# Second model of a fused two-model kernel: the last rows of w_out and of the down projection, two residual norms, the outputs and the first two feed-forward blocks go token tile by token tile

## The chip, the cores and the metric

The kernel runs on one core of one Trainium2 chip. What counts is the time of one execution on the device in microseconds (us), median of the runs shown. The profile is one execution more, taken by the hardware profiler. Engines are named as in the profile: PE (TensorE), DVE (VectorE), ACT (ScalarE), POOL (GpSimd), SP (the queue that issues the loads of weights).

## The reference, cut to what matters

256 tokens of width 1024 go through two models of two layers each. The first model (adaptive modulation, three attention mixers, a convolutional feed-forward part) is not edited. A layer of the second model, cut to the parts that are:

```python
for l in range(DEPTH):
    h = rms_norm_2(x, norm_mix_pre[l])
    proj = h @ w_in[l]                      # latents, rope key, branches, gates
    ...
    merged = ...                            # gated sum of four branches
    x = x + rms_norm_2(merged @ w_out[l], norm_mix_post[l])
    h = rms_norm_2(x, norm_ffn_pre[l])
    u, g = jnp.split(h @ w_ffn_in[l], 2, axis=-1)      # 2 x 2816 columns
    x = x + rms_norm_2((silu(u) * g) @ w_ffn_out[l], norm_ffn_post[l])
```

## The kernel before

The 256 tokens are two tiles of 128. x lies token-major in SBUF, the normed x feature-major. Every matrix product is done on exact float32r parts: a = ah + al, and `mm3` (L178, L179, L180) adds ah·bh, ah·bl and al·bh. "Product" below is one such pass, one PE instruction. Weights come by SP's DMA into `wraw` tiles of 128x1024 (5 buffers); ACT casts the high part into `wh` (L259) and DVE subtracts to get the low part `wl` (L260), 5 buffers each. With a gain, a split is L262 on ACT and L263 on DVE.

No order of work is written out by hand. A scheduler takes the program as it is written, with its dependencies and buffers, and gives every engine one fixed list; an engine waits at the head of its list. `HOLD` names norms whose splits are to stand ahead of splits of weights: of the pieces that come behind the first `free`, `held` are issued only after the norm's split numbered `at`.

The places that the change and the prediction touch:

- Handover from w_out to the feed-forward part ("out to ffn", once a layer) and from the down projection to the next layer ("gpre", once). Both run the norm `add_normed` of the projection's output: sums of squares on ACT (L216), gain times accumulator on DVE (L1370), `rsqrt` on DVE (L189 to L202, 128x1 steps), addition to x (L1375), sums of squares of the new x, a second `rsqrt`, x times r (L232 on DVE, L233 on ACT), 8 transposes a tile on PE (L236), splits L262 and L263. The accumulators are four banks: two named acc for tile 0, ada and o for tile 1.
- The feed-forward part: 22 blocks of 128 hidden columns, weights stationary and 256 tokens moving, 48 products for the gate half and the value half each; silu L1348, product with the value half L1349.
- The end: the last norm, then two output DMAs (L1408) of 512 KB.
- Latents (behind gpre): 48 products into two acc banks, sums of squares L1030, the rope key's 48 products and its DVE steps L1023 and L1024, an `rsqrt` of 128x4 steps (L189, L207 to L211), L1036 times r, transposes L1043. None of these lines is edited.

Of the kernel before, what the change touches and what calls it, by code (L numbers as in the profile page):

```python
# [15 lines left out]
AF = mybir.ActivationFunctionType  # L16
# [29 lines left out]
# norms whose splits go ahead of the weight splits emitted before: of the pieces behind the first `free`, `held` are issued  # L46
# only after the split numbered `at`
HOLD = dict(n11=(4, 6, 7), n20=(2, 6, 7), n21=(4, 6, 7), gpre=(2, 6, 7), gffn=(4, 6, 7))


class Core:
# [16 lines left out]
    # tag: (columns, slots) of the small and the short-lived tiles, which lie side by side in one; those of a block share their place  # L68
# [20 lines left out]
    def tile(self, shape, dtype, tag):  # L89
        """a tile of a ring"""  # L90
# [13 lines left out]
    BUFS = dict(T=20, xo=5, wraw=5, wh=5, wl=5, v4=3)  # L104

    def wide(self, tag, dtype=F32):
        """a [P, 1024] tile"""
        self.n += 1
        return self.pool.tile([P, 1024], dtype, tag=tag, name=f"{tag}_{self.n}", bufs=self.BUFS[tag])

    def pair(self):
        """two [P, 512] tiles side by side"""
        t = self.wide("T", F32R)
        return t[:, :512], t[:, 512:]
# [33 lines left out]
    def queue(self, ins, before):  # L148
        """ins is issued after before, on the same engine"""
# [3 lines left out]
    def weights(self, flat, key, layer, k0, nk, starts, width, piece=1024):  # L153
        """columns (start, k, col) of a weight block as exact (high, low) float32r parts"""
# [27 lines left out]
    def rsqrt(self, parts, n, inv_n):  # L182
        """(sum(parts) * inv_n + EPS) ** -0.5, n columns"""
# [12 lines left out]
        # a cubic step and Newton's, each short of a factor: s goes from -1 to -8/3 to 1024/27, which cancels big ** -0.5  # L196
# [22 lines left out]
    def norm_to(self, x, dst, col, gain, shift=None, sums=None, site=None, tiles=((0, 1),)):  # L219
        """x: two token-major [P, D] tiles -> dst[k] = (h, l) feature-major at columns col..col+256, rms-normed, *gain (+shift).  # L220
        sums: per tile, sums of squares of x's parts where these are already there."""
        self.norm_split(self.normed(x, sums), dst, col, gain, shift, site, tiles)

    def normed(self, x, sums=None):
        """rms-normed x, feature-major, in banks of two blocks"""
# [29 lines left out]
    def split(self, src, h, l, gain=None, shift=None):  # L255
        """src (PSUM or SBUF, fp32) * gain + shift -> h + l."""
# [15 lines left out]
    def transpose_split(self, blocks, dsts):  # L272
        """blocks: SBUF [P, P] pieces -> dsts (h, l) [P, P * len(blocks)]"""
# [8 lines left out]
class Block1:  # L282
# [22 lines left out]
    def ada(self, l):  # L305
        """modulation rows of a layer, a bank of four 512-column chunks at a time: [sh1|sc1], [gt1|sh2], [sc2|gt2];
        a chunk's rows lie at partitions 32g (x, 16 copies) and 32g + 16 (ctx). Yields after each step."""
# [38 lines left out]
    def mod_col(self, v, gain=None):  # L346
        """[P, 2, 4, 32] view (PSUM) -> per stream [P, 8]: the values, or (1 + values) * gain"""
# [11 lines left out]
    def gate_rows(self, l, n, s):  # L359
        """a stream's gate 1 or 2 on every partition, [P, 1024]"""  # L360
# [7 lines left out]
    def tables(self, l):  # L368
        """rope tables with the gains: t = q * TA + swap(q) * TB on (first half, second half) dims."""
# [49 lines left out]
    def in_chunk(self, l, name, XT, full):  # L419
        """256 columns of x @ w_in: per stream a psum view [P, 2 token tiles, 256]"""  # L420
# [14 lines left out]
    def qk(self, kind, ps, nh, hd, s):  # L435
        """One stream's q or k heads, psum view [P, 2, nh*hd]: rms norm, rope and gain, then exact (high, low) parts, feature-major
        and stacked on the partitions so that few passes hold all terms of (qh + ql)(kh + kl) but ql kl:
          q 64: [qh; ql] (or [ql; qh] where the head's kl lies in the upper half), k 64: [kh; kh] and pairs of kl,
          q 32: [qh; ql; qh], k 32: [kh; kh; kl].
        Tiles hold two heads of 256 tokens each."""  # L440
# [81 lines left out]
    def scores(self, q, k, unit):  # L522
        """psum [P queries, 512]: one x token tile against all 512 keys, or two ctx tiles against the 256 ctx keys each.
# [373 lines left out]
class Block2:  # L897
# [94 lines left out]
    def layer(self, l):  # L992
# [331 lines left out]
        for u in range(0, KD, 2):  # L1324
            out_proj(u)
# [218 lines left out]
```

## Time and profile before

| | |
|---|---|
| three runs | 2209.02, 2211.74, 2217.74 us; median 2211.74 |
| the profiled execution, first to last instruction | 2206.8 us: 4.9 below the median, 2.2 below the fastest run |
| PE busy | 2121.0 us (96%) |
| DVE busy | 1491.9 us (68%) |
| ACT busy | 1073.9 us (49%) |
| mean granted TensorE clock | 0.976 of full speed |

The profiled execution's own time is its span. A clock of 1.00 is the level of 2.4 GHz and 0.50 that of 1.2 GHz; a mean in between is the share of a stretch at either.

### The profile page before, as it was taken

Reading aid. Unit: us, or ns where it says so; the run is one execution under the profiler, and the core shown is the slowest. Engines: PE = TensorE matmul, PEld = TensorE weight load, DVE = VectorE, ACT = ScalarE, POOL = GpSimd, SP = SyncE. Lnnn points to the kernel's source line nnn. Section 1 sums busy time; section 2 is a strip of 40 time slices with the busy share of each in tenths; the row PEclk is TensorE's granted clock in tenths of the full one; section 3 lists DMA queues with packets and bytes.
Section 4 is the critical chain, followed back from the end, with each engine's and each line's share of the span. In section 5 each row is a group of like instructions: output and inputs, shape, how many; then the busy total and the mean of one; then the engine's idle time right before and its main releaser. Section 6 shows DMA issues by size and latency. Waiting matters only on the chain.

```text
span 2206.8 us, 35818 instructions
## 1 busy us (share of the span) xinstructions
PE 2121.0 (96%) x14204; PEld 1859.2 (84%) x14204; DVE 1491.9 (68%) x3008; ACT 1073.9 (49%) x1841; POOL 0.8 (0%) x7
## 2 busy tenths in 40 slices
PE   6999999899999999998999999998998999998998
PEld 3785667788888898788998899998997999997997
DVE  5663556855556686678777889866555879976454
ACT  4443453532333364566556644455444654454443
POOL 0000000000000000000000000000000000000000
PEclk9998999899999998999999999999999999999999
DMA  9344555322323331034554445554553545554662
GB/s 342 110 163 138 187 189 177 136 76 97 108 77 124 104 99 53 25 123 164 176 200 160 153 163 192 191 182 145 190 184 127 172 153 163 184 190 145 189 183 76
DMA packets 94839, 331.63 MB, mean 150 GB/s; under 512 B 10928, under 2 KB 11312, under 8 KB 94544
## 3 DMA queue, kind: packets, MB, share of 16 engines
q1 hardware_dynamic: 94672, 329.35, 45.5%
q8 instruction: 111, 1.82, 0.3%
q14 instruction: 56, 0.46, 0.1%
HBM read 328.20 MB, written 1.11 MB: 149 GB/s over the span
## 4 chain that ended last, share of the span: by engine, by line
PE 91%; DVE 6%; ACT 2%; DMA 1%; issue 1%; DVEq 0%; ACTq 0%
PE ps L178 17%; PE ps L179 17%; PE ps L180 16%; PE acc L178 6%; PE acc L179 6%; PE acc L180 6%; PE ps L533 4%; PE ada L318 3%; PE o L574 2%; PE ps L558 2%; PE ada L179 1%; PE ada L178 1%; PE ada L180 1%; PE o L179 1%; PE o L178 1%; PE o L180 1%
## 5 line engine op out<-in xcount | busy, mean ns | idle before, releaser
L178 PE MATMUL ps<-T,wh 128*128 128x256 f32 (+1 forms) x2640 | 787.4, 299 | 1.1 <-ACT T L262 1.1
L179 PE MATMUL ps<-T,wh 128*128 128x256 f32 (+1 forms) x2640 | 785.8, 298 | 0.4 <-DVE T L263 0.4
L180 PE MATMUL ps<-T,wl 128*128 128x256 f32 (+1 forms) x2640 | 784.5, 298 | 0.0
L260 DVE TENSOR_TENSOR wl<-wraw,wh 128x1024 fp32r<-128x1024 f32 (+1 forms) x514 | 608.8, 1201 | 157.6 <-ACT wh L259 90.8
L259 ACT CAST wh<-wraw 128x1024 fp32r<-128x1024 f32 (+1 forms) x514 | 515.8, 1031 | 234.6 <-PE ps L179 77.4
L178 PEld LDWEIGHTS ps<-T,wh 128*128 128x128 f32 x2640 | 506.1, 192 | 18.5 <-ACT T L262 2.1
L179 PEld LDWEIGHTS ps<-T,wh 128*128 128x128 f32 x2640 | 506.4, 192 | 17.3 <-DVE T L263 1.3
L180 PEld LDWEIGHTS ps<-T,wl 128*128 128x128 f32 x2640 | 506.2, 192 | 13.8
L178 PE MATMUL acc<-wh,T 128*128 128x256 f32 (+1 forms) x988 | 314.2, 319 | 3.5 <-ACT T L265 3.1
L179 PE MATMUL acc<-wl,T 128*128 128x256 f32 (+1 forms) x988 | 313.1, 318 | 2.3 <-DVE wl L260 2.3
L180 PE MATMUL acc<-wh,T 128*128 128x256 f32 (+1 forms) x988 | 311.5, 316 | 0.3 <-DVE T L269 0.3
L178 PEld LDWEIGHTS acc<-wh,T 128*128 128x128 f32 x988 | 190.3, 193 | 19.4 <-ACT T L265 3.5
L180 PEld LDWEIGHTS acc<-wh,T 128*128 128x128 f32 x988 | 189.9, 192 | 14.7 <-DVE arena L189 1.3
L179 PEld LDWEIGHTS acc<-wl,T 128*128 128x128 f32 x988 | 190.6, 193 | 13.9 <-DVE wl L260 3.0
L542 DVE TENSOR_REDUCE arena<-ps 128x1 f32<-128x512 f32 (+1 forms) x100 | 67.5, 686 | 78.9 <-PE ps L533 78.5
L1141 DVE SCALAR_TENSOR_TENSOR arena<-arena 128x241 f32<-128x241 f32 (+14 forms) x240 | 113.2, 474 | 3.7
L259 ACT CAST T<-arena 128x256 fp32r<-128x256 f32 (+2 forms) x128 | 58.8, 468 | 96.3 <-PE ps L179 26.7
L533 PEld LDWEIGHTS ps<-T,T 128*128 128x128 f32 (+2 forms) x320 | 59.3, 200 | 54.1 <-issue 29.2
L533 PE MATMUL ps<-T,T 128*128 128x256 f32 (+2 forms) x320 | 100.9, 386 | 2.1 <-ACT T L517 2.1
L318 PE MATMUL ada<-wraw,arena 128*32 128x512 f32 x384 | 86.9, 636 | 11.6 <-DVE arena L293 8.3
L546 ACT ACTIVATE arena<-ps,arena 128x512 f32<-128x512 f32 (+1 forms) x120 | 73.6, 620 | 48.1 <-DVE arena L542 37.5
L260 DVE TENSOR_TENSOR T<-arena,T 128x256 fp32r<-128x256 f32 (+2 forms) x128 | 63.2, 501 | 48.8 <-ACT T L259 48.4
(226 smaller groups left out, 2219.1 us busy)
## 6 DMA issues: line engine op xcount, KB each, us to landing
wraw<-w SPq DMA_DIRECT2D x586, 512.0 KB, 4.0
wraw<-w SPq DMA_DIRECT2D x22, 256.0 KB, 2.9
xo<-row SPq DMA_DIRECT2D x12, 256.0 KB, 6.2
v<-xin SPq DMA_DIRECT2D x4, 512.0 KB, 8.5
arena<-rpb SPq DMA_DIRECT2D x8, 256.0 KB, 2.7
v<-post SPq DMA_DIRECT2D x4, 512.0 KB, 4.4
arena<-bada SPq DMA_DIRECT2D x6, 256.0 KB, 5.4
arena<-bc SPq DMA_DIRECT2D x2, 768.0 KB, 4.0
```

The costliest lines, as they stand in the source:

```text
L178: mm(out, ah, bh, start=start, stop=False)
L179: mm(out, ah, bl, start=False, stop=False)
L180: mm(out, al, bh, start=False, stop=stop)
L259: a = nc.scalar.copy(h, src)
L260: b = nc.vector.tensor_tensor(l, src, h.bitcast(F32), op=ALU.subtract)
L318: nc.tensor.matmul(ps[32 * g : 32 * g + 32, :], self.cT[:, k].rearrange("p s r -> p (s r)"), raw[g // 2][0][:, g % 2 * 512 : g % 2 * 512 + ...
L533: self.nc.tensor.matmul(ps[:, col : col + 256], a[:, c], b, start=(n == 0), stop=(n == len(q[s]) - 1))
L542: nc.vector.tensor_reduce(m, ps.rearrange("p (t k) -> p t k", t=nt), axis=AX, op=ALU.max, negate=True)
L546: nc.scalar.activation(p[:, c], ps[:, c], AF.Exp, bias=m[:, i : i + 1], accum_out=tot[:, i : i + 1])
L558: nc.tensor.transpose(ps[:, b * P : b * P + P], p[:, b * P : b * P + P], K.ident)
L574: self.nc.tensor.matmul(out[64 * i : 64 * i + 64, t * P : t * P + P], v[:, k, cols[i] : cols[i] + 64], pts[i][:, b * P : b * P + P], start ...
L1141: yield v.scalar_tensor_tensor(y[:, lo:hi], zs[j][:, lo + t - 15 : hi + t - 15], self.cfw[:, j, t : t + 1], y[:, lo:hi], op0=ALU.mult, op1 ...
```

## The change

- `rows`, a new method, does the last four row blocks of w_out and of the down projection together: 24 products for token tile 0, then 24 for tile 1, and of the last two row blocks those of the first column half before those of the second. Before, two row blocks went at a time, tile 0 and tile 1 by turns.
- `add_normed` takes the sums of squares of a tile directly ahead of that tile's norm, and in the last layer sends each half of a tile out by a DMA of its own (four of 256 KB).
- The feed-forward norm's splits go tile by tile (16 of 128 columns where 8 of 256 were), and its `HOLD` entry follows.
- The first two feed-forward blocks are done together and token-major: normed tokens stationary, 256 weight columns moving, 48 products for tile 0, then 48 for tile 1; silu and product per tile, two transposes a tile (L1345) bring the result back.
- `wh` and `wl` have 7 buffers where 5 were, in both models.

The lines of the diff that do something (the rest removes comments):

```diff
-HOLD = dict(n11=(4, 6, 7), n20=(2, 6, 7), n21=(4, 6, 7), gpre=(2, 6, 7), gffn=(4, 6, 7))
+HOLD = dict(n11=(4, 6, 7), n20=(2, 6, 7), n21=(4, 6, 7), gpre=(2, 6, 7), gffn=(4, 4, 15))
-    BUFS = dict(T=20, xo=5, wraw=5, wh=5, wl=5, v4=3)
+    BUFS = dict(T=20, xo=5, wraw=5, wh=7, wl=7, v4=3)
...
-        for u in range(0, KD, 2):
+        for u in range(0, KD - 4, 2):
             out_proj(u)
+        out_proj(KD - 4, 4)
         sums = self.add_normed(acc, 0)
-        K.norm_to(x, H, 0, sm["gffn"], sums=sums, site="gffn")
+        K.norm_to(x, H, 0, sm["gffn"], sums=sums, site="gffn", tiles=((0,), (1,)))
...
+        get = [K.weights(wname, "w_ffn_in_2", l, 0, KD, [c], 256) for c in (0, FT * P)]
+        ft = K.bank()
+        for t in range(2):
+            ps = K.bank()
+            for i in range(2):
+                for k in range(KD):
+                    h, lo = H[k]
+                    K.mm3(ps[:, i * 256 : i * 256 + 256], (h[:, t * P : t * P + P], lo[:, t * P : t * P + P]), get[i](k * 256, 256), k == 0, k == KD - 1)
+            s = K.tmp()
+            act(s[:, :256], ps[:, :256], AF.Silu)
+            v.tensor_tensor(s[:, 256:], s[:, :256], ps[:, 256:], op=ALU.mult)
+            for j in range(2):
+                nc.tensor.transpose(ft[:, j * 256 + t * P : j * 256 + t * P + P], s[:, 256 + j * P : 256 + j * P + P], K.ident)
...
-            if j % 2 == 1 and j >= 3:
+            if j % 2 == 1 and j < FT - 1:
                 down(j - 3)
-        down(FT - 2)
+        down(FT - 4, 4)
+    def rows(self, acc, wname, key, X, a, n, last):
+        K = self.K
+        get = [K.weights(wname, key, self.l, a + i, 2, [0], 1024) for i in range(0, n, 2)]
+        order = [(f, cc) for f in range(n - 2) for cc in range(2)] + [(f, cc) for cc in range(2) for f in (n - 2, n - 1)]
+        for t in range(2):
+            c = slice(t * P, t * P + P)
+            for f, cc in order:
+                h, lo = X[a + f]
+                K.mm3(acc[t, cc], (h[:, c], lo[:, c]), get[f // 2](f % 2 * 1024 + cc * 512, 512), a + f == 0, a + f == last - 1)
...
-        parts = [[K.sumsq(acc[t, cc]) for cc in range(2)] for t in range(2)]
         for t in range(2):
-            tm = []
+            parts, tm = [], []
             for cc in range(2):
+                parts.append(K.sumsq(acc[t, cc]))
...
+                else:
+                    nc.sync.dma_start(self.ap["out"][t * P : t * P + P, c], xc)
```

What the change does to the engines' lists is seen at three places. The first is DVE's list at out to ffn of the second layer; the names are those above, ada and o being tile 1's accumulators. Before:

```order
L1370 TENSOR_TENSOR arena<-ada_19427,v_2316_19573 128x512
L1375 SCALAR_TENSOR_TENSOR arena<-arena 128x512 x2
L1370 TENSOR_TENSOR arena<-o_19428,v_2316_19573 128x512
L189 TENSOR_SCALAR arena<-arena 128x1 x2
L191 SCALAR_TENSOR_TENSOR arena<-arena 128x1 x2
```

After the change (L1390 and L1396 are the former L1370 and L1375):

```order
L1390 TENSOR_TENSOR arena<-ada_19448,v_2317_19594 128x512
L189 TENSOR_SCALAR arena<-arena 128x1
L1390 TENSOR_TENSOR arena<-o_19449,v_2317_19594 128x512
L191 SCALAR_TENSOR_TENSOR arena<-arena 128x1
L200 SCALAR_TENSOR_TENSOR arena<-arena 128x1
L197 TENSOR_SCALAR arena<-arena 128x1
L201 SCALAR_TENSOR_TENSOR arena<-arena 128x1
L198 SCALAR_TENSOR_TENSOR arena<-arena 128x1
L202 SCALAR_TENSOR_TENSOR arena<-arena 128x1
L199 SCALAR_TENSOR_TENSOR arena<-arena 128x1
L232 TENSOR_SCALAR xo_19632<-arena 128x512
```

Tile 0's second `rsqrt` (of its new x) has moved forward among tile 1's first steps: here L200, L201, L202 and L232 are tile 0's, and its L189 to L199 stand directly ahead of the first row. Before, the two tiles' `rsqrt` went in pairs.

The second place is PE's list of the second layer after the change, at the end of tile 0's 48 products of the first two feed-forward blocks (ps_19735 is tile 0's bank, ps_19788 tile 1's, ps_19734 the transposes'):

```order
L178 MATMUL ps_19735<-wh_19730,T_19631 128x256
L179 MATMUL ps_19735<-wl_19731,T_19631 128x256
L180 MATMUL ps_19735<-wh_19730,T_19631 128x256
L1345 MATMUL ps_19734<-arena 128x128 x2
L178 MATMUL ps_19788<-wh_19714,T_19628 128x256
```

Tile 0's two new transposes stand directly behind its products and ahead of tile 1's. All 16 transposes L236 of the norm stand ahead of the first product, as before.

The third place is DVE's list behind gpre of the second layer, at the latents' `rsqrt`, which no edited line touches. Before:

```order
L260 TENSOR_TENSOR wl_16496<-wraw_16489,wh_16495 128x1024
L189 TENSOR_SCALAR arena<-arena 128x4
L207 TENSOR_SCALAR arena<-arena 128x4
L209 TENSOR_TENSOR arena<-arena 128x4
L210 SCALAR_TENSOR_TENSOR arena<-arena 128x4
L211 SCALAR_TENSOR_TENSOR arena<-arena 128x4
L209 TENSOR_TENSOR arena<-arena 128x4
L260 TENSOR_TENSOR wl_16504<-wraw_16499,wh_16503 128x1024
L210 SCALAR_TENSOR_TENSOR arena<-arena 128x4
L211 SCALAR_TENSOR_TENSOR arena<-arena 128x4
```

After the change:

```order
L260 TENSOR_TENSOR wl_16529<-wraw_16522,wh_16528 128x1024
L207 TENSOR_SCALAR arena<-arena 128x4
L260 TENSOR_TENSOR wl_16694<-wraw_16689,wh_16693 128x1024
L209 TENSOR_TENSOR arena<-arena 128x4
L210 SCALAR_TENSOR_TENSOR arena<-arena 128x4
L260 TENSOR_TENSOR wl_16698<-wraw_16691,wh_16697 128x1024
L211 SCALAR_TENSOR_TENSOR arena<-arena 128x4
L209 TENSOR_TENSOR arena<-arena 128x4
L1023 TENSOR_TENSOR arena<-ps_16410,arena 128x512
L210 SCALAR_TENSOR_TENSOR arena<-arena 128x4
L1024 TENSOR_TENSOR arena<-arena 128x256
L211 SCALAR_TENSOR_TENSOR arena<-arena 128x4
```

In the shown part three subtractions stand where one stood, with the rope key's two steps among them; a fourth (wl_16706) follows the last row, ahead of the last three steps of the `rsqrt` and of L1036. Before, L1023, L1024 and the next subtraction stood behind L1036. The first layer's list has changed in the same way.

## Rows read from the trace of the kernel before

**Rows 1.** The page: engines' busy time, and the chain that ended last, by engine.

```profile
PE 2121.0 (96%) x14204; PEld 1859.2 (84%) x14204; DVE 1491.9 (68%) x3008; ACT 1073.9 (49%) x1841; POOL 0.8 (0%) x7
...
PE 91%; DVE 6%; ACT 2%; DMA 1%; issue 1%; DVEq 0%; ACTq 0%
```

**Rows 2.** Waits of PE: waiting line, releaser, us in total, times, longest.

```profile
PE ps L236 <- DVE arena L189: 20.9, 3, 7.4
```

**Rows 3.** Windows: stretch, length, busy time of each engine, granted clock, DMA.

```profile
851.00:864.40 13.40, 12.23 (x35) 7.20 (x34) 3.40 (x7) 3.14 (x7) 0.00 (x0) 0.65 0.07 20
905.70:915.40 9.70, 9.70 (x66) 6.71 (x65) 5.79 (x16) 4.71 (x11) 0.00 (x0) 1.00 0.06 20
1191.90:1200.00 8.10, 4.16 (x19) 3.58 (x20) 6.52 (x28) 4.96 (x15) 0.00 (x0) 0.79 0.37 115
1692.50:1705.00 12.50, 5.71 (x22) 4.92 (x22) 10.24 (x41) 8.03 (x24) 0.00 (x0) 0.59 0.18 54
1997.40:2012.20 14.80, 6.86 (x31) 6.46 (x32) 11.87 (x41) 8.31 (x22) 0.00 (x0) 0.65 0.33 107
```

**Rows 4.** Timeline at out to ffn, second layer: start, us, engine, line, [idle before].

```profile
1997.51 0.60 ACT L216 ACTIVATE arena<-o 128x512 f32<-128x512 f32 x1
...
2000.36 0.68 DVE L1370 TENSOR_TENSOR arena<-o,v 128x512 f32<-128x512 f32 x1
...
2002.87 1.41 DVE L1375 SCALAR_TENSOR_TENSOR arena<-arena 128x512 f32<-128x512 f32 x2
```

**Rows 5.** Timeline of PE at the same place.

```profile
2004.73 1.97 PE L236 MATMUL ps<-arena,xo 128*128 128x128 f32 x8 [7.36 <-DVE arena L189]
2007.31 1.97 PE L236 MATMUL ps<-arena,xo 128*128 128x128 f32 x8 [0.61 <-DVE xo L232]
2008.93 0.56 PE L178 MATMUL ps<-T,wh 128*128 128x256 f32 x1
```

**Rows 6.** Groups of the tile ps, 1505 to 1520 us: duration ns min/median/max.

```profile
L1348 ACT ACTIVATE arena<-ps x2: 384/384/384, 1512.3 to 1517.3; 128x256 f32<-128x256 f32 x2
L1349 DVE TENSOR_TENSOR arena<-arena,ps x2: 421/421/421, 1512.7 to 1517.7; 128x256 f32<-128x256 f32 x2
```

**Rows 7.** Timeline of DVE at the latents, second layer.

```profile
1715.97 0.16 DVE L189 TENSOR_SCALAR arena<-arena 128x4 f32<-128x4 f32 x1
...
1717.08 1.23 DVE L260 TENSOR_TENSOR wl<-wraw,wh 128x1024 fp32r<-128x1024 f32 x1
1718.22 0.16 DVE L210 SCALAR_TENSOR_TENSOR arena<-arena 128x4 f32<-128x4 f32 x1
...
1719.28 1.66 DVE L1036 TENSOR_SCALAR arena<-acc,arena 128x256 f32<-128x256 f32 x4
...
1721.98 0.69 DVE L1023 TENSOR_TENSOR arena<-ps,arena 128x512 f32<-128x512 f32 x1
...
1722.97 0.42 DVE L1024 TENSOR_TENSOR arena<-arena 128x256 f32<-128x256 f32 x1
```

**Rows 8.** Timeline of PE at the latents.

```profile
1720.62 1.04 PE L1043 MATMUL ps<-arena 128*128 128x128 f32 x8
1722.22 0.51 PE L178 MATMUL ps<-T,wh 128*128 128x256 f32 x2 [0.56 <-ACT T L262]
1722.56 0.40 PE L178 MATMUL ps<-wh,T 128*128 128x512 f32 x1
1722.79 0.39 PE L179 MATMUL ps<-wl,T 128*128 128x512 f32 x1
```

**Rows 9.** Timeline of DVE and ACT at the end.

```profile
2194.72 0.69 DVE L1370 TENSOR_TENSOR arena<-acc,v 128x512 f32<-128x512 f32 x1 [6.49 <-ACT arena L216]
...
2201.72 1.41 DVE L1375 SCALAR_TENSOR_TENSOR arena<-arena 128x512 f32<-128x512 f32 x2
...
2197.50 0.60 ACT L216 ACTIVATE arena<-o 128x512 f32<-128x512 f32 x1
```

**Rows 10.** Timeline in the first model: a subtraction on DVE, a wait of PE.

```profile
781.61 1.22 DVE L260 TENSOR_TENSOR wl<-wraw,wh 128x1024 fp32r<-128x1024 f32 x1
...
852.40 0.78 PE L512 MATMUL ps<-ident_r,xo 128*128 128x128 f32 x5 [1.17 <-DVE xo L466]
```

More of the change, by code (lines that the diff above doesn't have):

```diff
@@ L1247, in layer, with out_proj @@
         acc = {}
-        def out_proj(u):
-            get = K.weights(wname, "w_out_2", l, u, 2, [0], 1024)
-            for t in range(2):
-                for k in range(2):
-                    h, lo = M[u + k]
-                    for cc in range(2):
-                        K.mm3(acc[t, cc], (h[:, t * P : t * P + P], lo[:, t * P : t * P + P]), get(k * 1024 + cc * 512, 512),
-                              u + k == 0, u + k == KD - 1)
+        def out_proj(u, n=2):
+            self.rows(acc, wname, "w_out_2", M, u, n, KD)
         YC = self.halves(4)
@@ L1323, in layer, with down @@
         acc.update(zip([(t, cc) for t in range(2) for cc in range(2)], K.acc4()))
-        for u in range(0, KD, 2):
+        for u in range(0, KD - 4, 2):
             out_proj(u)
+        out_proj(KD - 4, 4)
         sums = self.add_normed(acc, 0)
         H = self.halves(KD)
-        K.norm_to(x, H, 0, sm["gffn"], sums=sums, site="gffn")
+        K.norm_to(x, H, 0, sm["gffn"], sums=sums, site="gffn", tiles=((0,), (1,)))
         acc = dict(zip([(t, cc) for t in range(2) for cc in range(2)], K.acc4()))
         F = {}
-        def down(a):
-            get = K.weights(wname, "w_ffn_out_2", l, a, 2, [0], 1024)
-            for t in range(2):
-                for f in range(2):
-                    h, lo = F[a + f]
-                    for cc in range(2):
-                        K.mm3(acc[t, cc], (h[:, t * P : t * P + P], lo[:, t * P : t * P + P]), get(f * 1024 + cc * 512, 512), a + f == 0, a + f == FT - 1)
-        for j in range(FT):
+        def down(a, n=2):
+            self.rows(acc, wname, "w_ffn_out_2", F, a, n, FT)
+        get = [K.weights(wname, "w_ffn_in_2", l, 0, KD, [c], 256) for c in (0, FT * P)]
[11 more added lines that the diff above has]
+                nc.tensor.transpose(ft[:, j * 256 + t * P : j * 256 + t * P + P], s[:, 256 + j * P : 256 + j * P + P], K.ident)
+        hv = self.halves(2)
+        for j in range(2):
+            F[j] = hv[j]
+            K.split(ft[:, j * 256 : j * 256 + 256], *F[j])
+        for j in range(2, FT):
             get = K.weights(wname, "w_ffn_in_2", l, 0, KD, [j * P, (FT + j) * P], P)
@@ L1364, in add_normed @@
         sums = []
-        parts = [[K.sumsq(acc[t, cc]) for cc in range(2)] for t in range(2)]
         for t in range(2):
-            tm = []
+            parts, tm = [], []
             for cc in range(2):
+                parts.append(K.sumsq(acc[t, cc]))
                 tm.append(K.tmp())
                 v.tensor_tensor(tm[cc], acc[t, cc], gain[:, cc * 512 : cc * 512 + 512], op=ALU.mult)
-            r = K.rsqrt(parts[t], 1, 1.0 / D)
+            r = K.rsqrt(parts, 1, 1.0 / D)
             out = []
             for cc in range(2):
-                xc = self.x[t][:, cc * 512 : cc * 512 + 512]
+                c = slice(cc * 512, cc * 512 + 512)
+                xc = self.x[t][:, c]
                 v.scalar_tensor_tensor(xc, tm[cc], r, xc, op0=ALU.mult, op1=ALU.add)
@@ L1406 @@
         b2.layer(l)
-    for t in range(2):
-        nc.sync.dma_start(ap["out"][t * P : t * P + P, :], x[t])
     specs.update(K.specs)
```

## Prediction

> **What bounds the kernel now.** I read the page first: PE is busy 96% of the span and holds 91% of the chain that ended last [rows 1]. So a change can gain only where PE stands still or runs at the lower clock, and it loses wherever it makes PE stand still anew. The waits of PE say where: the largest group is 20.9 us in three waits for a small DVE step of a norm [rows 2], which are the two handovers out to ffn and gpre. The windows around two of them show the second cost: the granted clock is 0.65 over 14.8 us and 0.59 over 12.5 us [rows 3], that is, 10.4 and 10.2 us of each stretch at 1.2 GHz, reached after PE had stood idle. Last I read the timelines: what stands between PE's last product and its next transposes at the handover [rows 4, 5], at the latents behind gpre [rows 7, 8], and at the end [rows 9].
>
> Let T be the end of the last product ahead of a handover. In the second layer's out to ffn the transposes start at 2004.73 after 7.36 us idle, so T is 1997.37; tile 1's transposes start at T+9.94 and the first product at T+11.56 [rows 5].
>
> **Out to ffn.** Products of 512 columns follow each other in 0.23 us [rows 8], so `rows` closes tile 0's accumulators 24 x 0.23 = 5.5 us ahead of T, and tile 0's norm runs beside tile 1's products. Yet PE's next product comes only behind all 16 transposes, so tile 1 decides. Its way after the change: ACT's sums of squares of ada and o stand behind those of tile 0's new x, and o's ends at about T+2.6; DVE's product with the gain (0.68 [rows 4]) at T+3.3; its `rsqrt`, shared with tile 0's second one and a 0.49 scaling, at T+5.3; the two additions (1.41 [rows 4]) at T+6.6; the second sum of squares at T+7.6; another `rsqrt` and the scaling at T+9.6. All these are sums of durations of the kind shown in [rows 4], placed in the order that DVE's list now has. Before, DVE had o's product with the gain only at 2000.36, T+3.0, and the additions at T+5.5 [rows 4]: tile 1 was late for the same kind of reason. So tile 1's transposes move from about T+9.9 to T+9.6: a gain of 0.3 at most, and about 0.2 in the first layer. The idle time stays over 7 us, so I keep the lower clock as it is.
>
> The two token-major blocks have 96 products, as two blocks had before. New are four transposes, 4 x 0.13 = 0.5 (eight took 1.04 [rows 8]). And the first two stand ahead of tile 1's products in PE's list: PE waits there for silu and product, 0.38 and 0.42 [rows 6] and some 0.2 of hand-overs: 1.0 us, if ACT and DVE are free. Tile 1's two stand 12 products into the next block, and those hide them. Sum per handover: -0.2 + 0.5 + 1.0 = +1.3, for two layers **+2.6**. Tile 0's splits, 16 narrow ones now, lie beside tile 1's wait; they cost nothing while that wait is over 2.5 us.
>
> **gpre.** The same chain without the weights' subtraction in it brings tile 1's transposes forward by about **0.3**, once between the layers. The last rows' first products hide the last feed-forward block's split, 24 products ahead of the ones that need it.
>
> **End.** With T = 2197.36 (the sum of squares of o starts 0.14 behind the product in [rows 4], and at 2197.50 here [rows 9]) the last addition ends at 2203.13, T+5.77. Afterwards it is: sum of squares to T+0.9, gain, `rsqrt`, two additions, some T+4.4: **-1.35**. The 3.7 us from there to the end of the span are the output transfer and stay; half-size transfers could save part of it, which I count as nothing. Here a row and a rule meet: DVE's product with the gain had been idle 6.49 us and began only when ACT's sum of squares of the same bank had been read (2194.72 [rows 9]), though both only read. The Trainium skill, "PSUM — Partial Sum Buffer", section "PSUM bank collisions raise a hardware error", says that two engines may not be in one bank and quadrant at once, reads included, and that the scheduler adds a dependency between them; the trace agrees. By it the pairing per tile in the source starts nothing earlier, and the end is T+4.4; without it, T+3.8 and 0.6 us more of gain.
>
> **The latents, which no edited line touches.** Seven buffers let ACT cast weights further ahead, and DVE's list takes the subtractions as they come. Behind gpre they now stand inside the latents' `rsqrt`: four in it where one was, and the rope key's L1023 and L1024 too, which stood behind it. The first step is at 1715.97 and L1036 at 1719.28 [rows 7]; PE had no wait, its transposes started at 1720.62 directly behind the rope key's products [rows 8]. A subtraction takes 1.14 us of the list (1717.08 to 1718.22), L1023 0.60 and L1024 0.35 of the list [rows 7]. L1036 moves by 3 x 1.14 + 0.60 + 0.35 = 4.4 us, to about 1723.7, and L1023 itself must first wait for the rope key's end at 1720.7, some 0.2 more. L1036 ended 0.7 us ahead of the end of the transposes (1720.94 against 1721.66), so these now end at about 1726.0, 4.3 later; the two stalls behind them (0.56 is one [rows 8]) shrink by about 0.3, since L1023 no longer stands ahead of the splits. That is **+4.0** in each layer, a PE idle of some 3.6 us. The bounds are 2.5, if one subtraction's cast is late and DVE is idle anyway, and 5. An idle of about that size stands in the windows between the two models: 1191.9 to 1200.0 has a clock of 0.79, so 3.4 us at the lower level [rows 3], worth up to 1.7 us. Part of it falls into the wait: I take **+1.0** in each layer. Two layers: **+10.0**.
>
> **First model.** The same deeper casting moves subtractions there too. Two of 1.1 us leave norm chains that PE waits for (one is the row at 781.61 [rows 10]): -2.2. The wait of 1.17 at 852.40 [rows 10] finds 22 more products ahead of it: -1.2. One norm chain has three subtractions more ahead of it and two fewer in it: +1.1. Together **-2.3**; bounds -6 and +5, since runs of scores there change their mixture of work.
>
> **Sum.** 2.6 - 0.3 - 1.35 + 10.0 - 2.3 = +8.65 on the profiled span of 2206.8: 2215.4. That execution lies 4.9 below the median of the runs, so in runs I expect 2211.7 + 8.7 = **2220.4 us**, +0.4%.
>
> **Rivals.**
>
> *A, slower beyond doubt.* The latents' chain as above, and besides a run of scores in the first model's second layer at the lower clock. The decisive point is whether score work without weight products keeps the clock: 851 to 864.4 ran at 0.65, 9.4 us at the lower level, 905.7 to 915.4 with about as many instructions at 1.00 [rows 3]. After the change two longer runs without products stand there. If one more loses 9.4 us to half speed it costs up to 4.7: +13.4, 2225; if both, 2230. For it: the first window. Against it: the second, and that the first began behind a wait which now goes.
>
> *B, the latents are not held up.* If the casts are late by the buffers of `wraw`, which stay 5, the subtractions come when DVE would be idle, but a list keeps its order, so DVE then waits inside the chain all the same. Only if they are all early enough to be done before 1715.97 is the term near zero: 8.65 - 10.0 = -1.35, 2210.4, no change to be measured. For it: DVE's wait for casts at this place in the old list. Against it: the rope key's products hold the buffers until 1720.6.
>
> *C, faster.* Tile 0's early norm takes tile 1's off the path: transposes at T+6.7 instead of T+9.6 (if DVE's list were not full of tile 0's steps) gives -2.9 at each out to ffn, -2 at gpre, and with the idle shorter, the clock's loss of some 1.3 us each in three places: 8.65 - 5.8 - 2 - 3.9 = -3; with the latents as in B, -13, 2199. The point is where tile 1's sums of squares stand in ACT's list. Against it: the order shown.
>
> *D, the change does nothing of what it sets out to do, and nothing else:* handover terms cancel, latents half: within 5 us of before, 2214 or so.
>
> **How the numbers follow.** A difference of 0.5%, 11 us, is about what a measurement of this kernel can tell from none. My forecast has 0.50, A 0.18, B 0.12, C 0.08, D 0.12. The forecast's own spread (2214 to 2226) reaches over the bound at 2222.8 for about a third. Slower: A, and 0.17 of the forecast: 0.35. Faster (under 2200.7): C and little of B: 0.09. The same: 0.56. The range 2204 to 2229 leaves out most of C and A's far end.
>
> **What would show it.** In the trace after the change: tile 1's transposes L236 about 9.6 us behind the last product and the clock still near 0.65; a wait of about 1 us at the first L1345; the span's end 8.1 us behind the last product where it was 9.44; L1043 waiting 3 to 4 us for L1036 in both layers, with DVE full of L260 ahead of it. The prediction is wrong if L1043 does not wait, if the wait at L1345 is several us because ACT or DVE have casts queued there, or if the first model moves by more than 5 us either way.

## The result, and the profile after

| | before | after |
|---|---|---|
| median of the runs | 2211.1 us (4 runs) | 2237.0 us (3 runs, 2236.0 to 2237.9) |
| the profiled execution | 2206.8 us | 2235.1 us |
| mean granted clock | 0.976 | 0.969 |

The ratio of the runs is 1.0111, with an interval from 1.0088 to 1.0135: 1.1% slower, beyond the range and on the side that had 0.35. (A fourth run after the change took 4119 us and is left out.) On the page of the profile PE is as busy as in [rows 1], and longer:

```profile
span 2235.1 us, 35877 instructions
PE 2142.8 (96%) x14212; PEld 1874.0 (84%) x14212; DVE 1498.0 (67%) x3024; ACT 1083.3 (48%) x1857; POOL 0.8 (0%) x7
```

PE's busy time grew by 21.8 us and its idle time by 6.5, so most of the loss is not idle time at all. The waits of PE (line waited for, total, times, longest) answer to [rows 2]:

```profile
PE ps L236 <- DVE xo L232: 32.6, 10, 4.2
...
PE ps L1043 <- DVE arena L1036: 6.9, 2, 3.4
PE ps L276 <- DVE xo L671: 6.8, 1, 6.8
PE ps L236 <- DVE arena L199: 4.7, 1, 4.7
...
PE ps L1345 <- DVE arena L1343: 2.2, 2, 1.2
```

The latents' wait L1043 and the token-major blocks' L1345 are new, as forecast; the 6.8 us at L276, in the first model, are new too, and not forecast.

Where the 28.3 us arose is read by matching products: every version has 11,856 products, so the starts of the two traces' products of one number give the shift there, and the difference of two such shifts the loss of the stretch between.

| stretch (us in the trace of before) | lost | forecast |
|---|---|---|
| 0 to 430, both programs in the first model | +3.6 | none |
| 430 to 830, first model | -1.7 | -2.3, with the next row |
| 830 to 1052, first model, second layer | +7.7 | |
| 1190 to 1262, latents, layer 0 | +6.4 | +5.0 |
| 1262 to 1436, attention and branches, layer 0 | +3.6 | none |
| 1496 to 1690, out to ffn, layer 0 | +1.1 | +1.3 |
| gpre between the layers | 0.0 | -0.3 |
| 1722 to 1788, latents, layer 1 | +7.4 | +5.0 |
| to 1997, branches, layer 1 | +1.8 | none |
| out to ffn, layer 1 | +0.7 | +1.3 |
| end | -2.2 | -1.35 |

The first 3.6 us differ between executions, not between programs: the run e1 below, whose first model is that of before, shows 4.0 there in its profiled execution, the run e12 -0.7, and the run e3, whose first model is that of after, -0.3. What is left, some 24.7 us, is the change's as far as one execution can tell, against a forecast of 8.65. Of the 6.4 of the latents in layer 0, 0.9 arise ahead of them, at layer 0's first norm, where 6.8 us ran at half clock behind a wait of 3.87 (3.4 us in the kernel before, behind the same wait); e3 has the order of after there, the same wait, and 3.4 us, so this part too differs between executions.

**First model.** The windows of the stretch between the same two products (columns as in [rows 3]), first before, then after with three stretches in it:

```profile
830.90:1039.20 208.30, 195.15 (x1410) 170.42 (x1409) 150.38 (x401) 119.72 (x246) 0.00 (x0) 0.94 0.27 87
```

```profile
832.80:1048.80 216.00, 201.07 (x1411) 174.38 (x1410) 151.04 (x401) 120.15 (x247) 0.00 (x0) 0.91 0.26 84
859.40:869.70 10.30, 10.30 (x29) 6.91 (x28) 5.29 (x18) 1.45 (x4) 0.00 (x0) 0.50 0.19 51
900.40:907.20 6.80, 6.80 (x28) 5.37 (x29) 3.49 (x12) 2.56 (x6) 0.00 (x0) 0.50 0.00 0
917.50:924.30 6.80, 6.80 (x21) 4.89 (x21) 2.67 (x7) 2.04 (x7) 0.00 (x0) 0.50 0.00 0
```

PE's idle time grew from 13.15 to 14.93 us, by 1.8; its busy time by 5.9. A mean clock of 0.94 over 208.3 us is some 25 us at 1.2 GHz, 0.91 over 216.0 some 39. In three stretches after the change PE did score work, with a few weight products in it, without a pause at half clock. Of the idle time, 6.83 us stand at one place where before had 1.05. PE's rows there, before:

```profile
986.89 0.44 PE L276 MATMUL ps<-arena,xo 128*128 128x128 f32 x2 [1.05 <-DVE xo L671]
1000.73 2.58 PE L236 MATMUL ps<-arena,xo 128*128 128x128 f32 x11 [6.99 <-DVE arena L202]
```

After, DVE's timeline and PE's rows:

```profile
991.59 0.15 DVE L209 TENSOR_TENSOR arena<-arena 128x4 f32<-128x4 f32 x1
991.66 1.22 DVE L260 TENSOR_TENSOR wl<-wraw,wh 128x1024 fp32r<-128x1024 f32 x1
992.79 0.15 DVE L210 SCALAR_TENSOR_TENSOR arena<-arena 128x4 f32<-128x4 f32 x1
992.87 1.22 DVE L260 TENSOR_TENSOR wl<-wraw,wh 128x1024 fp32r<-128x1024 f32 x1
994.00 0.15 DVE L211 SCALAR_TENSOR_TENSOR arena<-arena 128x4 f32<-128x4 f32 x1
994.08 1.22 DVE L260 TENSOR_TENSOR wl<-wraw,wh 128x1024 fp32r<-128x1024 f32 x1
995.21 0.42 DVE L670 TENSOR_TENSOR xo<-xo,arena 128x256 f32<-128x256 f32 x1
995.66 0.42 DVE L671 TENSOR_TENSOR xo<-xo,arena 128x256 f32<-128x256 f32 x1
```

```profile
996.14 0.48 PE L276 MATMUL ps<-arena,xo 128*128 128x128 f32 x1 [6.83 <-DVE xo L671]
1010.29 1.94 PE L236 MATMUL ps<-arena,xo 128*128 128x128 f32 x8 [4.70 <-DVE arena L199]
```

These small steps are the `rsqrt` of a second norm chain, that of the differential attention's heads; weight subtractions stand between its steps. But they stood there before too: from its first step (L666) to the end of L671 the chain takes 10.73 us with seven subtractions in it, before 8.91 with six. What changed more is PE's list: between the instruction whose result starts the chain (L652) and L276 it has 32 instructions, 3.99 us of work, where before had 65 with 7.95. Of the 5.8 us by which the wait grew, 1.8 are the longer chain and 4.0 the work that no longer covers it. The wait behind it, that of the residual norm, is 4.70 where before had 6.99.

**Latents.** DVE and PE, second layer, answering to [rows 7, 8]:

```profile
1736.63 0.17 DVE L189 TENSOR_SCALAR arena<-arena 128x4 f32<-128x4 f32 x1 [0.46 <-ACT arena L1030]
1736.71 1.23 DVE L260 TENSOR_TENSOR wl<-wraw,wh 128x1024 fp32r<-128x1024 f32 x1
...
1737.92 1.22 DVE L260 TENSOR_TENSOR wl<-wraw,wh 128x1024 fp32r<-128x1024 f32 x1
...
1739.33 1.22 DVE L260 TENSOR_TENSOR wl<-wraw,wh 128x1024 fp32r<-128x1024 f32 x1
...
1741.37 0.69 DVE L1023 TENSOR_TENSOR arena<-ps,arena 128x512 f32<-128x512 f32 x1 [0.55 <-PE ps L180]
...
1742.52 1.22 DVE L260 TENSOR_TENSOR wl<-wraw,wh 128x1024 fp32r<-128x1024 f32 x1
...
1744.23 1.66 DVE L1036 TENSOR_SCALAR arena<-acc,arena 128x256 f32<-128x256 f32 x4
```

```profile
1744.77 2.32 PE L1043 MATMUL ps<-arena 128*128 128x128 f32 x8 [3.44 <-DVE arena L1036]
```

```profile
1743.50:1753.70 10.20, 8.36 (x30) 6.97 (x31) 6.78 (x16) 4.14 (x8) 0.00 (x0) 0.50 0.02 6
1231.50:1238.30 6.80, 6.24 (x24) 5.26 (x22) 4.49 (x8) 4.14 (x8) 0.00 (x0) 0.50 0.00 0
```

The chain is the forecast one, piece for piece, and its wait of 3.44 us too (3.6 had been forecast). The price is the first row below it: 10.2 us at half clock, with 8.36 us of PE's work in them, of which about half is lost time: by this estimate up to 4.2 us, where 1.0 had been taken. The second row is layer 0, where the wait is 3.44 us too and 6.8 us follow at half clock.

**Out to ffn**, second layer, PE, answering to [rows 5], and **the end**, DVE and ACT, answering to [rows 9]:

```profile
2031.38 1.97 PE L236 MATMUL ps<-arena,xo 128*128 128x128 f32 x8 [4.19 <-DVE xo L232]
2036.24 1.97 PE L236 MATMUL ps<-arena,xo 128*128 128x128 f32 x8 [2.90 <-DVE xo L232]
2046.22 0.44 PE L1345 MATMUL ps<-arena 128*128 128x128 f32 x2 [0.98 <-DVE arena L1343]
```

```profile
2228.70 0.69 DVE L1390 TENSOR_TENSOR arena<-o,v 128x512 f32<-128x512 f32 x1 [0.61 <-ACT arena L216]
...
2230.78 1.41 DVE L1396 SCALAR_TENSOR_TENSOR arena<-arena 128x512 f32<-128x512 f32 x2
...
2227.98 0.60 ACT L216 ACTIVATE arena<-o 128x512 f32<-128x512 f32 x1 [0.67 <-PE o L180]
2228.47 0.19 ACT L216 ACTIVATION_READ_ACCUMULATOR arena<-o 128x1 f32 x1
```

The last product ended at 2027.19, so tile 1's transposes start at T+9.05 (forecast T+9.6, before T+9.94). At the end of the program T is 2227.84 and the last addition ends at T+4.35 (forecast T+4.4).

**Branches.** What loads PE's stationary operand waits for ACT's tanh (L1264, before L1270) 10 times in the layer-0 stage, 3 times before; the two rows are the weight loads' waits, before and after:

```profile
PEld ps L178 <- ACT arena L1270: 0.5, 3, 0.2
```

```profile
PEld ps L178 <- ACT arena L1264: 2.2, 10, 0.4
```

PE is busy for 110.54 of 110.9 us at a clock of 1.00 in this stretch (1327.4 to 1438.3; before 108.7 of 108.7, 1310.1 to 1418.8), so of the 2.2 us lost here little is idle time and none is the clock's. One of the waits in ACT's timeline: a cast for a later block stands ahead of the tanh, and waits for its weights.

```profile
1375.42 1.05 ACT L259 CAST wh<-wraw 128x1024 fp32r<-128x1024 f32 x1 [1.99 <-DMA wraw<-w]
1376.38 0.46 ACT L1264 ACTIVATE arena<-ps,arena 128x256 f32<-128x256 f32 x1
```

### The profile page after: what moved, and what is told of

Same layout as the page of the kernel before. It is cut to its first block, busy times and chain, and to the rows that moved or that the text cites. A ratio compares the mean times of both kernels' runs of the same rounds, so it can differ in the third digit from the quotient of the medians.

```text
span 2235.1 us, 35877 instructions
## 1 busy us (share of the span) xinstructions
PE 2142.8 (96%) x14212; PEld 1874.0 (84%) x14212; DVE 1498.0 (67%) x3024; ACT 1083.3 (48%) x1857; POOL 0.8 (0%) x7
## 4 chain that ended last, share of the span: by engine, by line
PE 88%; DVE 6%; ACT 2%; DMA 2%; issue 1%; DVEq 0%; ACTq 0%; SPq 0%
PE ps L178 16%; PE ps L179 16%; PE ps L180 16%; PE acc L178 6%; PE acc L180 6%; PE acc L179 6%; PE ps L533 4%; PE ada L318 3%; DMA wraw<-w 2%; PE o L574 2%; PE ps L558 2%; DVE wl L260 1%; PE ada L180 1%; PE ada L178 1%; PE ada L179 1%
## 5 line engine op out<-in xcount | busy, mean ns | idle before, releaser
L178 PE MATMUL ps<-T,wh 128*128 128x256 f32 (+1 forms) x2576 | 771.2, 300 | 1.5 <-ACT T L262 1.1
L179 PE MATMUL ps<-T,wh 128*128 128x256 f32 (+1 forms) x2576 | 767.7, 298 | 0.6 <-DVE T L269 0.5
L180 PE MATMUL ps<-T,wl 128*128 128x256 f32 (+1 forms) x2576 | 765.5, 298 | 0.0
L178 PEld LDWEIGHTS ps<-T,wh 128*128 128x128 f32 x2576 | 494.2, 192 | 21.6 <-ACT arena L1264 4.3
L179 PEld LDWEIGHTS ps<-T,wh 128*128 128x128 f32 x2576 | 494.3, 192 | 17.2 <-DVE T L269 1.6
L180 PEld LDWEIGHTS ps<-T,wl 128*128 128x128 f32 x2576 | 493.4, 192 | 14.1
L178 PEld LDWEIGHTS acc<-wh,T 128*128 128x128 f32 x988 | 192.6, 195 | 19.8 <-ACT T L265 3.8
L180 PEld LDWEIGHTS acc<-wh,T 128*128 128x128 f32 x988 | 192.3, 195 | 15.2 <-DVE arena L268 1.5
```

Of the source, the lines that this page charges most:

```text
L178: mm(out, ah, bh, start=start, stop=False)
L179: mm(out, ah, bl, start=False, stop=False)
L180: mm(out, al, bh, start=False, stop=stop)
```

## The experiments

The theory was that the buffers, not the reordered lines, cost the time, and that they do it by subtractions in DVE's chains; the rivals were casts on ACT, the reordered lines themselves, and the clock.

**The two halves of the change apart.** e1 is the changed kernel with the old depth, e2 the kernel before with the new one:

```diff
-    BUFS = dict(T=20, xo=5, wraw=5, wh=7, wl=7, v4=3)
+    BUFS = dict(T=20, xo=5, wraw=5, wh=5, wl=5, v4=3)
```

> The changed kernel with wh and wl back at 5 buffers, all of the token-tile order kept. Theory one (the two deeper buffers lose the time, by subtractions of weights that run ahead into chains of small DVE steps, and by the lower clock behind the waits so made): the first model's +9.5 us, the latents' +7.5 in each layer and the branch stage's +2 in each layer go; what is left is out to ffn +1 to +3 a layer and the end -2: 2209 to 2216 us, no wait at L1043. Rival (the token-tile order itself loses it, by the waits at L1345 and by more idle at the handovers): 2225 us or more.

> The kernel before with wh and wl at 7 buffers and nothing else. Theory one: nearly the whole loss, 2233 to 2240 us, with L1043 waiting 3 to 4 us in both layers and the first model 8 to 10 us longer. Rival: within 5 us of the kernel before, 2206 to 2216.

e1: 2214.7 us, ratio 1.0017 (1.0007 to 1.0027). Between 430 and 1436 us its shift stays within 0.2 us; the rest of the program loses 1.9 and 2.1 at out to ffn and 1.0 at gpre, and gains 2.2 at the end. e2: 2234.2, ratio 1.0105 (1.0091 to 1.0119), with L1043 waiting 3.44 and 3.64, L276 6.83, the branches +3.2 and +1.9. So seven buffers alone cost about 1%, and the rows, norms, outputs and blocks that the change is named for cost 0.2%.

**Only the high parts deeper** (`wh` 7, `wl` 5), and **the subtractions kept out of the latents' chain**: in e3, four subtractions and the rope key's L1023 and L1024 are queued on DVE behind L1036.

```diff
+            if self.behind is not None:
+                self.since += 1
+                if 3 < self.since <= 7: self.queue(pair[1], self.behind)
...
+        K.queue(v.tensor_tensor(kr, krp, self.rope[:, 512:], op=ALU.mult), last)
```

> The changed kernel with wh at 7 buffers and wl at 5: ACT may cast ahead, DVE may subtract no further ahead than before. If the subtractions in the chains are what costs (theory one): 2209 to 2217 us, as with 5 and 5. If the casts that run ahead on ACT cost as much (rival): 2225 or more.

> The changed kernel (7 buffers) with the latents' chain protected: the four subtractions behind the third piece and the rope key's two steps are issued only after L1036. Theory one, that the order on DVE and not the number of buffers as such makes the wait: L1043 does not wait, the clock stays up there, each layer is 7 to 8 us shorter, 2221 to 2224 us; the first model stays 9.5 longer than before. Rival (the buffers cost by themselves, through the loads of weights or through SBUF traffic): 2233 or more, or the wait moves to the next weights that are needed.

e4: 2231.7, 1.0089 (1.0073 to 1.0104). The latents' chain is short again (longest wait of L1043 0.6), but the theory's 2209 to 2217 failed. The first model lost 10.0 from 830 to 1052, the branches 4.4 and 2.3 (the weight loads' waits for L1264 are 2.4 us in 9 times), and tile 0's transposes came 6.17 us after the last product instead of 4.19. So the deeper `wh` alone, with `wl` as deep as before, costs 20 us of the 26. In the first model it is all clock: the stretch of 208.3 us takes 218.2 (835.9 to 1054.1) with PE idle for 13.3, as long as before, a clock of 0.90, and a wait of only 1.45 at L276. e3: 2220.5, 1.0043 (1.0029 to 1.0056): L1043 no longer waits, and 16 us of 26 are back. By matched products the latents gain 1.7 and 0.3 against the kernel before, where the changed kernel lost 6.4 and 7.4: 15.8 together.

**Seven in the second model only**, five in the first (e5), and with the latents held as in e3 (e6):

```diff
+        i, self.slot = self.slot, (self.slot + 1) % self.deep
+        return [self.wide(t if i < 5 else t + "2", F32R) for t in ("wh", "wl")]
...
+    K.slot, K.deep = 0, 7
```

> The changed kernel with wh and wl 5 deep in the first model and 7 deep in the second (a ring of 5 and one of 2). Theory one (the depth in the first model alone makes its 8 to 10 us, by other lists for PE, ACT and DVE there): the first model is as long as before, the latents' wait stays whole in the second layer and is shorter in the first, where the list has two subtractions in the chain and not four: 2224 to 2230 us. Rival (the first model's loss is a matter of the execution, not of the lists): 2234 or more.

> As the run before, and the latents' chain protected too. If the two places are the whole loss and add up: 2210 to 2215 us, with a granted clock that drops only where it did before. If the deeper buffers cost elsewhere (the branch stage took 2 us a layer more): 2215 to 2219.

e5: 2226.0, 1.0063 (1.0047 to 1.0079); e6: 2216.5, 1.0019 (1.0009 to 1.0028). e5 lies 10.9 us below the changed kernel. By matched products 5.9 of that is the first model behind 430 us, where e5 loses 0.1, and some 3.7 the latents of layer 0, which lose less there (L1043 waits 1.4 in two pieces). e6 lies 9.5 below e5, and by matched products the latents make up nearly all of that. In e6 the branches still lose 4.5 and 2.5, with 2.5 us of weight loads waiting for L1264 in layer 0.

**The first model.** e10 paces the casts of the second layer (each chunk's behind a copy on ACT three chunks earlier), e11 is e3 with the weight subtractions kept out of the differential attention's last chain too (the edit acts in both layers), e13 does both:

```diff
+            pair = self.split(t[:, :w], h[:, :w], l[:, :w]); self.after and self.queue(pair[0], self.after)
...
+            K.behind, K.since, K.first = nc.vector.tensor_tensor(v3(oc), v3(oc), self.gsub.unsqueeze(1).to_broadcast([P, n // 64, 64]), op=ALU.mult), 0, 4
```

> The changed kernel (7 buffers everywhere), but in the first model's second layer ACT casts a chunk's weights only behind the copy that empties the accumulators of the chunk three before, so that products are not drawn ahead of the scores. Theory (weights ready early draw products out of the attention, long runs of scores are left, and the clock falls there): the attention's 5 us come back, the norm chain behind it keeps its 2: 2230 to 2233 us, with fewer us at the lower clock between 855 and 960. Rival (the deeper buffers cost there in another way): 2236 or more.

> The run e3_latents_held, and in the first model's second layer the weight pieces that stood inside the differential attention's last sub-norm chain are queued behind that chain's last instruction. The first theory (most of the first model's loss is that this chain has subtractions 1024 wide in it): the wait of L276 falls from 6.83 to about 1, the norm after it waits some 6 to 7 instead of 4.70, and the time falls from 2220.5 by 4 to 6 us, to 2214.5 to 2217. The rival (the loss there has another cause, as the lower clock that the attention left behind): the wait of L276 may go, but the time stays at 2219 or above, since the products behind run at half clock as before.

> The run e11_both_chains_held, and the weight casts of the first model's second layer paced as in e10_paced_first (a chunk's casts queued on ACT behind the copy three chunks before). The theory that two things add up in the first model, the attention's mixture of score work and weight products and the sub-norm chain: the shift over the attention stage falls from some 4.6 to 11 us to under 1, the wait of L276 stays at or below 4.3, and the time falls from 2218.5 to 2213 to 2216. The rival (one loss that only moves between the two places, since weight work finished in the attention is missing as cover at the sub-norm chain): the shift behind both places stays at 7 us or more and the time at 2217 to 2220.

e10: 2235.7, 1.0113 (1.0097 to 1.013), as slow as the changed kernel, so that its theory's 2230 to 2233 failed: from 830 to 939 us it lost 0.4 where the changed kernel lost 4.6, but L276 waited 6.83 again, and by 1052 it had lost 6.7. e11: 2218.5, 1.0049 (1.0035 to 1.0062), which the intervals do not tell apart from e3, so that its theory's 4 to 6 us failed. Its chain has one subtraction left and takes 4.51 us, and yet L276 waits 4.26, now at 985.65: PE's list has no work at all between the chain's start and L276, and the weight products that stood there come behind it. e13: 2219.9, 1.0042 (1.0027 to 1.0058). Its shift is -1.8 us at 830, 1.3 at 939, 11.8 at 980 and 8.7 behind both places: the rival holds, the loss moves. The same stretch of PE's list in e13:

```profile
829.10:1047.90 218.80, 202.68 (x1411) 176.35 (x1410) 152.66 (x402) 120.72 (x247) 0.00 (x0) 0.90 0.24 81
```

16.1 us idle and a clock of 0.90, 44 us at half. And e3 and e2, whose first models are in the order of the changed kernel's, needed 219.7 us at 0.88 and 214.5 at 0.91 there, against 216.0 at 0.91: one order of work differs by 5.2 us between executions, so a difference of a few us in this stretch, from one execution each, tells nothing apart. Five deep, eight versions have the order of before there: six needed 208.3 us, among them the kernel before, e1 and e12, e6 needed 210.0 and e8 207.0. The two groups do not overlap.

**The handovers, carried through.** In e7 (five buffers) PE's list has tile 0's products ahead of tile 1's transposes, which the change did not do, and both tiles' transposes back (L1345) stand behind all products of the two blocks. e8 is e6 so, e9 is e7 with the latents held, e12 is e9 with layer 0's first norm made as before.

```diff
+            if t: self.norm_tile(H, sm["gffn"], 1, sums, "gffn")
...
+        for k in range(KD):
+            nc.tensor.transpose(ps[k // 4][:, k % 4 * P : k % 4 * P + P], xn[:, k * P : (k + 1) * P], K.ident)
```

> Buffers of 5, and the handovers' norms written tile by tile: tile 0's transposes and splits, tile 0's products, then tile 1's transposes, with two banks a tile; the four new transposes come behind tile 1's products. Theory: what the token order leaves unused is PE's wait of 2.3 to 3.1 us between the two tiles' transposes and the wait at L1345; products fill them: 3 to 4 us less at each of three handovers, 2201 to 2206 us. Rival: tile 0's splits and its products' weights delay tile 1's chain on DVE by as much, or the early products run at the lower clock: 2210 to 2216.

> The norms tile by tile, with 7 buffers in the second model only and the latents' chain protected. Fewer subtractions stand in the handovers' chains than with 5 buffers (one instead of three): 1 to 2 us less at each out to ffn than the run before, against some 2 us a layer in the branch stage: 2199 to 2206. Rival: no difference from the run before beyond 2 us.

> The tile-by-tile norms with buffers of 5, and the latents' chain protected from the subtractions. In the run without this protection the handovers were 1.5 to 2 us shorter than before, but the latents behind gpre cost 4.9 and 3.5 us. Theory: that was again subtractions and the rope key's steps ahead of L1036; protected, the two layers come back by 3 to 4 us each: 2204 to 2208 us. Rival (tile 1's later transposes push the latents themselves, so that the wait stays whatever stands in the chain): 2211 to 2214.

> The run e9_tile_by_tile_held, with layer 0's pre-norm of the gated stage made for both token tiles at once again, as in the kernel before. The theory: that norm tile by tile cost 3.5 us in e9, since its early products came at half clock, and so the time falls from 2209.3 to 2205 to 2207. The rival: the lower clock belongs to the idle time ahead of the norm, whichever way it is made, and the time stays at 2208 to 2211.

e7: 2212.9, 1.0008 (0.9999 to 1.0017), so that its theory's 2201 to 2206 failed. Out to ffn gained 1.8 and 1.5 us against before, but the first norm and the latents lost 4.9 in layer 0, where L1043 waited 1.88, and 3.5 in layer 1. e8: 2212.8, 1.0009 (0.9998 to 1.002), no different from e7 (its theory, 2199 to 2206, failed too), with the branches' loss. e9: 2209.3, 0.999 (0.9981 to 0.9999), between its theory's 2204 to 2208 and its rival's 2211 to 2214. e12: 2207.1, 0.9978 (0.9966 to 0.9989), 0.2% faster than the kernel before; its median is 2.2 below e9's, at the edge of the theory's span, though the two intervals overlap. By matched products the first norm and the latents of layer 0 lost 3.5 in e9 and 0.1 in e12, and out to ffn gains 1.5 and 2.1 in e12. Its PE at out to ffn of the second layer, and the windows of layer 0's first norm in e9 and in e12:

```profile
2000.42 1.97 PE L1392 MATMUL ps<-arena,xo 128*128 128x128 f32 x8 [5.56 <-DVE xo L1389]
```

```profile
1194.90:1208.00 13.10, 8.66 (x33) 6.74 (x33) 9.76 (x32) 8.66 (x21) 0.00 (x0) 0.74 0.26 81
```

```profile
1191.30:1204.40 13.10, 9.06 (x41) 7.50 (x41) 11.02 (x38) 9.97 (x27) 0.00 (x0) 0.87 0.36 116
```

PE stands still for 5.56 us once, with no wait over 0.6 us behind it at out to ffn, where the kernel before stood 7.36. And PE's wait in layer 0's first norm is 3.87 us in both, but 6.8 us of the one window are at half clock (0.74) and 3.4 of the other (0.87). That the tile-by-tile order makes this difference is not shown: the changed kernel and e3, with one order there and the same wait, differ in the same way (0.74 from 1199.0 to 1212.1, 0.87 from 1198.9 to 1212.0).

## Why the prediction was wrong

**The step that failed is the first model's.** It counted stalls: two subtractions out of norm chains (-2.2), one wait covered (-1.2), one chain longer (+1.1); in place of -2.3 the stretches from 430 us on lost 6.0. The first two terms came as far as they can be read: the subtraction at 781.61 is out of its chain, PE's wait there fell from 2.62 to 1.20 and the stretch gained 2.0 (the other one stands near 410 us, in the part that differs between executions), and the wait of 1.17 [rows 10] is gone. The third was forecast for the residual norm, whose wait got shorter instead; the three subtractions stand at the end of the chain ahead of it, the differential attention's, which had no wait worth naming before (1.05) and 6.83 after: +3.5 for the two together. For this chain the step looked at DVE's list only, and of the 5.8 us that its wait grew 4.0 come from PE's, which has less work left to cover it. Above all, of the 7.7 us lost from 830 to 1052 only 1.8 are idle time; 5.9 are PE's work at the lower clock. The prediction had this as its rival A, with 0.18 and up to 4.7 for each stretch of scores, and kept it out of the sum because a stretch almost without products had run at 1.00 [rows 3]. That reading was weak: the two stretches that it sets side by side do not have "about as many instructions" but 35 in 13.4 us and 66 in 9.7. The sum was 8 us short here, and its own sign of being wrong, a first model that moves by more than 5 us, came true.

**A place that was not in the sum.** Attention and branches lost 5.4 us in two layers, 2.2 of it from 1325 to 1436, where the weight loads' waits for tanh grew by 1.7; that these waits make the loss is likely, not shown, and the rest was not followed further. The prediction asked where subtractions go on DVE's list and never where casts go on ACT's, though it said itself that seven buffers let ACT cast further ahead. e4 shows deeper casts alone to be enough for it, e1 that without them nothing is lost; every version with seven `wh` in the second model loses 3 us or more there in layer 0, every one with five (e1, e7, e9, e12) 0.1 at most.

**The latents: mechanism right, size off.** Wait 3.44 where 3.6 was forecast; +6.4 and +7.4 where 5.0 was. The term that was mis-sized is the clock's: 1.0, taken from a stretch with 3.4 us at the lower level [rows 3], against 6.8 and 10.2 us, worth up to some 3 and 4 us. The rows of out to ffn, 10.4 and 10.2 us [rows 3], were the better model. e3 shows that it is this chain: without it the wait is gone, and the stretch at half clock with it.

**The handovers: right.** Out to ffn forecast +1.3 each, measured +1.1 and +0.7: in the second layer tile 1's transposes came 0.9 us earlier than before, not 0.3, and the new transposes and their wait cost 1.6 (0.5 and 1.0 forecast). The clock there stayed, as said: 10.2 us at half speed again. With five buffers (e1) it was +1.9 and +2.1: tile 0's transposes then come 5.57 instead of 4.19 us after the last product, and tile 1's at T+9.87. So nearly all of the 0.9 is the deeper buffers', and the token order by itself moved tile 1's norm by less than 0.1. gpre: 0.0 for -0.3. The end: -2.2 for -1.35. The chain is as forecast to 0.05 us. The other 0.8 is the output transfer, counted as nothing: from the last addition to the end of the span 2.9 us, where it was 3.7 (2.9 to 3.0 in every version with four transfers, 3.7 in e2 with two). DVE's product with the gain starts at 2228.70, when ACT's sum of squares of the same bank and its accumulator read (0.19 from 2228.47) had ended at 2228.66; without that wait T+3.8 had been worked out. That is the dependency which the Trainium skill gives two engines in one bank and quadrant, reads included ("PSUM — Partial Sum Buffer", section "PSUM bank collisions raise a hardware error"), and the trace agrees.

**Rivals.** A came true, and with the branches and the clock behind the latents on top it went beyond its 2230. B and D are out: the latents were held up. C wanted tile 1's norm off the path, and looked for it in ACT's list. What the runs show is PE's list: the changed kernel's has tile 0's products behind tile 1's transposes; e12's has them ahead, PE no longer waits for tile 1, and it is 0.2% faster, with five buffers and the latents' chain held.

What stays open: which property of the deeper order makes the first model's attention run at the lower clock. Neither keeping the chain free nor pacing the casts nor both restored the 207 to 210 us of the five-buffer order. Shown is only that the depth does it (e1, e2, e5), and that the deeper `wh` is enough (e4).

## What to carry to other kernels

A deeper buffer is a change of every engine's list, not of memory: with a scheduler that fills idle slots it puts casts and subtractions ahead of, and between, short steps that TensorE waits for, on ACT as well as on DVE, and in parts of the program that no line of the edit touches. Price it by going through the short dependent chains of the whole program on both lists, and through the work on TensorE's own list that covers each of them, and try it by itself first: e2 would have shown the loss without any other edit. And price a new wait of some 3.5 us in front of dense work by the half-clock stretch behind it as well; here that was worth about as much again.

## What the runs showed of the hardware

- The clock fell without idle time ahead of it: in the three windows of 859 to 924 us above PE was busy throughout, with attention scores and few weight products, and ahead of them it stood still for 0.35 us once (at 909.51). In the kernel before, 905.7 to 915.4 [rows 3] had scores too and kept 1.00. In the 10.7 us ahead of that window PE did 9 weight products beside the scores, in the 10.4 us ahead of 900.4 after the change 3; but in the 13.4 us ahead of 859.4 it did 69, and the clock fell all the same. No rule comes out of these.
- Waits of one length did not cost alike: 3.44 us came with 6.8 us at half clock in layer 0 and with 10.2 in layer 1, the same 3.87 us with 3.4 (e12, e3) or 6.8 (e9, the changed kernel), and e3 and the changed kernel have one order of work there.
- Profiled executions of one order of work differed by up to 4.9 us in the first 430 us (e2 4.6, e3 -0.3 against before), and by 5.2 us in one stretch of some 216 (e2 214.5, e3 219.7), where the granted clock was 0.91 and 0.88 and PE idle for 14.3 and 14.0 us. So a difference of one execution in one stretch proves little; here conclusions rest on waits that repeat, and on medians of 3 to 12 runs of a version.
